# Out projection of a decoder layer: sets of 256 features in two half banks, or sets of 512 with a block of tokens in each bank

## The chip, the cores and the metric

The kernel runs on one core of a Trainium2 chip. The metric is the device time of one execution in microseconds (us). A core has five engines with queues of their own: TensorE (PE, matrix products; PEld is its weight load), VectorE (DVE), ScalarE (ACT), GpSimd (POOL) and SyncE (SP, which here issues nearly all DMAs). Products go to PSUM, which has eight banks of 128 x 512 float32.

## The reference

One decoder layer on 512 tokens of 2048 features, in float32. A mixer (pooling and attention, merged by gates) gives `merged`; the part around the change is

```
x = x + gate_a * (merged @ w_out)                      # w_out: 2048 x 2048
h = rmsnorm(x, norm_moe) * (1 + scale_m) + shift_m
logits = h @ w_router                                  # 16 experts
# top-2 experts of the best group, for each token
x = x + gate_m * sum_of_experts(h)
out = rmsnorm(x, norm_final)
```

The kernel keeps float32 accuracy with three products for each one: an operand is split into a high part (`hi`, rounded to the type fp32r) and a rest (`lo`), and hi x hi, hi x lo and lo x hi are summed.

## The kernel before

All of the program is a list of items (`Item`) that `run_items` walks through. An item has `split` (ScalarE writes the high part of 128x1024 weights, VectorE the rest; `split_tiles`), `mm` (its products) and lists of functions that come `before` the products, `now` (right behind them) or `after` (before the next item's products, behind the next split). With `split_ahead` 1 the order in which instructions are written out is: split of item i+1, `after` of item i-1, products of item i, `now` of item i, split of item i+2, `after` of item i, and so on. Every engine works its own instructions in that order. Two sets of split weights alternate (`parts`), so the split of item i+2 begins when the products of item i are over. Weights come in loads of 1 MB into three buffers in turn (`ring`); a load serves two items.

The out projection (`out_items`, `pair_items` with `token_major`) takes the 2048 output features 256 at a time: eight sets p of four items, 48 products an item. A stationary block is 128 tokens of `hh` or `hl` (the split `merged`); what streams is 256 columns of `w_out`, so a product is 128x256 (lines L645, L647, L648). A set has two banks, each of which holds two blocks of tokens side by side; sets alternate between banks 0, 1 and banks 2, 3 (`next_pair`). The set's `post` comes behind the next set's first splits: for each half, VectorE multiplies the bank by the row of `gate_a` (`ga`, L1049), adds x (`xr`, L1050), multiplies by the norm's row (`am`, L1051), and ScalarE sums the squares into `ssq2` (L1053). Two DMAs of 512 KB store z in `zrows` and the new x in `acc` (L1059). In the next set's items z is transposed (`z_turn`, L1068, copied by ScalarE, L1069), and the router's logits are summed (`logits`, L1077). The last set does this at once, half by half. x's columns are loaded a set ahead (`x_load`, L1037, L1040) by SyncE.

Meanwhile eight of the first expert's weight loads (1 MB each, L1154, L1155) go into tiles `craw`, one at every third item (`prefetch`). After the last logits comes the routing, a chain of small VectorE operations, at whose end GpSimd gathers the first expert's rows from `zrows` (L1213), and then 16 experts with weights streamed from memory (L1132, L1133, L1147).

The two lines that set where a set's evacuation stands and which banks it uses:

```
        items[-1].after.append(lambda: post(cell["ps"]))
        rot.update(ids=[0, 1], i=0)
```

Of the kernel before, what the change touches and what calls it, by code (L numbers as in the profile page):

```python
# [21 lines left out]
NB = T // P  # L22
KD = D // P
H = 8
E = 16
# [113 lines left out]
def trunk_kernel(ctx: ExitStack, tc: tile.TileContext, x, c, w_ada, b_ada, norm_mix, norm_moe, w_in,  # L139
# [32 lines left out]
    ssq2 = glob.tile([P, NB * 8], F32, name="ssq2")  # L172
# [55 lines left out]
    def bank(i):  # L228
        return psB.tile([P, 512], F32, name=f"bank{i}", tag=f"bank{i}")
# [404 lines left out]
                mm3(ps.tiles[j], hi[:, js], lo[:, js], mh[:, k + kk, :], ml[:, k + kk, :], k + kk == 0,  # L634
                    k + kk == nk - 1)

    def token_major(ps, k, hi, lo, ws, mh, ml, nk):

        for b in range(NB):
            o, bs = ps.tiles[b // 2][:, (b % 2) * 256:(b % 2) * 256 + 256], slice(b * P, (b + 1) * P)  # L640
            for kk in range(4):
                js = slice(ws[kk], ws[kk] + 256)
                sh, sl = mh[:, k + kk, bs], ml[:, k + kk, bs]

                pe.matmul(o, lhsT=sh, rhs=hi[:, js], start=k + kk == 0 and b % 2 == 0, stop=False,  # L645
                          skip_group_check=True)
                pe.matmul(o, lhsT=sh, rhs=lo[:, js], start=False, stop=False, skip_group_check=True)  # L647
                pe.matmul(o, lhsT=sl, rhs=hi[:, js], start=False, stop=k + kk == nk - 1, skip_group_check=True)  # L648

    def pair_items(w, col0, mh, ml, post, nk=KD, products=feature_major):  # L650

        items, cell = [], {}
        for q in range(nk // 8):
            def load(r, q=q):
                sp.dma_start(r.rearrange("p (k c) -> p k c", c=256),
                             w[q * 1024:(q + 1) * 1024, col0:col0 + 256].rearrange("(k p) c -> p k c", p=P))
                return r

            raw = Raw(load, 2)
            for hf in range(2):  # L660
                def split(raw=raw, hf=hf, q=q):
                    cell[q, hf] = split_tiles(raw.tile[:, hf * 1024:(hf + 1) * 1024], 1024)

                def mm(hf=hf, q=q):
                    if q == 0 and hf == 0:
                        cell["ps"] = next_pair()
                    hi, lo = cell.pop((q, hf))
                    products(cell["ps"], q * 8 + hf * 4, hi, lo, [0, 256, 512, 768], mh, ml, nk)
# [325 lines left out]
        slot += 1  # L994


    c_stack = ctx.enter_context(ExitStack())
    b3_stack = ctx.enter_context(ExitStack())
    b3, c_ = {}, {}
    lg_pair = {}  # L1000

    def open_b3():
        am_stack.close()
        g_stack.close()
        b3["pool"] = b3_stack.enter_context(tc.tile_pool(name="b3pool", bufs=1, side="left", reuse_waits="tile"))
        rot.update(ids=[0, 1], i=0)
        lg_pair["t"] = pair(3)
        c_["pool"] = c_stack.enter_context(tc.tile_pool(name="cpool", bufs=1, side="right", reuse_waits="tile"))
        c_["sh"] = c_["pool"].tile([P, D], F32, name="shrow")
        c_["gm"] = c_["pool"].tile([P, D], F32, name="gmrow")  # L1010
        for i, n in enumerate(("sh", "gm")):
            m = modd[i:i + 1].rearrange("s k p -> s (k p)")
            sp.dma_start(c_[n], m.to_broadcast([P, D]))

    def shift_logits():

        w3 = b3["pool"].tile([P, KD, E], F32, name="wshift")
# [9 lines left out]
    def b3_tile(name, n=1024):  # L1027
        return b3["pool"].tile([P, n], F32, name=name, tag=name, bufs=1)

    def out_items(p):  # L1030

        cell = {}
        ps_ = slice(p * 256, (p + 1) * 256)

        def x_load():
            cell["xr"] = xr = b3_tile("xr")
            sp.dma_start(xr.rearrange("p (b c) -> p b c", b=NB), x2d[:, ps_].rearrange("(b p) c -> p b c", p=P))  # L1037
            for i, n in ((2, "ga"), (3, "am")):
                cell[n] = b3_tile(n, 256)
                sp.dma_start(cell[n], modd[i:i + 1].rearrange("s k p -> s (k p)")[:, ps_].to_broadcast([P, 256]))  # L1040

        def post(ps):
            x2, z = cell["xr"], b3_tile("z")
            cell["z"] = z
            for hf in range(2):
                xs_ = slice(hf * 512, (hf + 1) * 512)
                v = {n: t[:, xs_].rearrange("p (b c) -> p b c", c=256) for n, t in (("x2", x2), ("z", z))}
                row = {n: cell[n][:, None, :].to_broadcast([P, 2, 256]) for n in ("ga", "am")}
                dve.tensor_tensor(v["z"], ps.tiles[hf].rearrange("p (b c) -> p b c", c=256), row["ga"], ALU.mult)  # L1049
                dve.tensor_add(x2[:, xs_], x2[:, xs_], z[:, xs_])  # L1050
                dve.tensor_tensor(v["z"], v["x2"], row["am"], ALU.mult)  # L1051
                for b in (2 * hf, 2 * hf + 1):
                    act.activation(b3_tile("junk", 256), x2[:, b * 256:(b + 1) * 256], AF.Square,  # L1053
                                   accum_out=ssq2[:, b * 8 + p:b * 8 + p + 1])
                if p == 7:
                    z_turn(hf)
                    logits(hf)
            for t, d in ((z, zrows), (x2, acc)):
                sp.dma_start(d[0:T, ps_].rearrange("(b p) c -> p b c", p=P), t.rearrange("p (b c) -> p b c", b=NB))  # L1059

        def z_turn(hf):

            ps, zT = bank(4 + hf), b3_tile(f"zT{hf}", 512)
            cell["zT", hf] = zT
            for j in range(2):
                for b in range(2):
                    o = (2 * hf + b) * 256 + j * P
                    pe.transpose(ps[:, (2 * j + b) * P:(2 * j + b + 1) * P], cell["z"][:, o:o + P], ident)  # L1068
            act.activation(zT, ps, AF.Copy)  # L1069

        def logits(hf):
            lg = lg_pair["t"][:, 512:512 + NB * E]
            for b in (2 * hf, 2 * hf + 1):
                for j in range(2):
                    k = 2 * p + j
                    o = (2 * j + b % 2) * P
                    pe.matmul(lg[:, b * E:(b + 1) * E], lhsT=cell["zT", hf][:, o:o + P],  # L1077
                              rhs=wr[:, k, :], start=k == 0 and b == 0, stop=k == KD - 1,
                              skip_group_check=True)

        it = pair_items(wout, p * 256, hh, hl, post, products=token_major)
        return it, x_load, z_turn, logits

    outs = [out_items(p) for p in range(8)]
    b3_items = []
    for p in range(8):
        it = outs[p][0]
        if p == 0:
            gates[-1].after += [open_b3, outs[0][1]]
        else:  # L1090
            for hf in range(2):
                it[1].after.append(lambda f=outs[p - 1][2], hf=hf: f(hf))
                it[2].after.append(lambda f=outs[p - 1][3], hf=hf: f(hf))
            it[1].after.append(outs[p][1])
        b3_items += it
    b3_items[0].after.append(shift_logits)
    b3_items[2].after.append(shift_sum)

    NCR, LSC, LEAD = 8, 2, 4
# [4 lines left out]
    def craw_tile(i):  # L1104
        return c_["pool"].tile([P, 2048], F32, name=f"craw{i}")
# [338 lines left out]
    dve.tensor_reduce(s4, ssq2.rearrange("p (b k) -> p b k", k=8), axis=AX.X, op=ALU.add)  # L1444
    newton_rstd(rs2, s4, t4)
    act.activation(sqrt_set, epst, AF.Exp)
    lg = rtile("lg")
# [279 lines left out]
```

## Time and profile before

| | |
|---|---|
| median of 3 runs | 2397.55 us (2397.06 to 2399.11) |
| the profiled execution | 2397.21 us, of it span 2395.5 us |
| TensorE busy | 2325.1 us, 97% of the span |
| VectorE, ScalarE busy | 1748.3 us, 1163.7 us |
| out projection | 1024.7 to 1227.8 us, TensorE busy 203.10 us |
| routing | 1227.8 to 1255.4 us |
| experts | 1255.4 to 2395.5 us |
| mean granted TensorE clock | 0.988 |

Span is from the first to the last instruction of the profiled execution. Busy time is a union over an engine's instructions. [...]

### The profile page before, as it was taken

The page shows a single profiled execution, that of the slowest core. Times are in us where ns is not written, and L with a number is a line of the kernel's source. Part 1 is how long each engine was busy: PE and PEld are TensorE (multiplying, and loading weights), DVE is VectorE, ACT ScalarE, POOL GpSimd, SP SyncE. Part 2 cuts the span into 40 slices and gives each one's busy share as a digit, 9 for nine tenths or more (in the row PEclk, how much of TensorE's full clock was granted, in tenths as well). Part 3 has the DMA queues.
Part 4 walks back from the last instruction along what each step waited for, and adds up shares of the span by engine and source line. Part 5 has one row for each costly group of instructions (what it writes and reads, how often), then busy time and mean ns, then how long its engine had stood idle before and what let it go on. Part 6 is the DMA issues. An engine that isn't in the chain of part 4 may idle for free.

```text
span 2395.5 us, 29296 instructions
## 1 busy us (share of the span) xinstructions
PE 2325.1 (97%) x11478; PEld 1929.4 (81%) x11478; DVE 1748.3 (73%) x1750; ACT 1163.7 (49%) x1070; POOL 127.7 (5%) x73
## 2 busy tenths in 40 slices
PE   7999999999999999999969999999999999999996
PEld 6888777788887888899968888888788888888883
DVE  7987333377665666343349999999999999999995
ACT  4323323322222222233227777777776777777775
POOL 0000100000000000000000111001101100100010
PEclk9999999999999999999979999999999999999998
DMA  9878724266665667366648999999998999999996
GB/s 338 277 245 205 101 71 71 71 234 240 237 233 192 236 233 256 108 201 196 222 152 314 347 372 384 399 384 368 371 381 345 376 411 366 372 378 376 376 359 264
DMA packets 269775, 662.57 MB, mean 277 GB/s; under 512 B 20084, under 2 KB 160620, under 8 KB 249708
## 3 DMA queue, kind: packets, MB, share of 16 engines
q1 hardware_dynamic: 262112, 641.89, 73.6%
q0 software_dynamic: 4752, 17.48, 3.0%
q8 instruction: 91, 1.49, 0.2%
q10 hardware_dynamic: 2768, 1.29, 0.2%
q14 instruction: 52, 0.43, 0.0%
HBM read 648.32 MB, written 29.39 MB: 283 GB/s over the span
## 4 chain that ended last, share of the span: by engine, by line
PE 77%; DMA 11%; DVE 7%; issue 3%; ACT 2%; POOL 0%; SPq 0%; POOLq 0%; DVEq 0%; ACTq 0%
PE bank L1147 27%; PE bank L242 10%; PE bank L244 10%; PE bank L243 10%; DMA G<-zrows,dest 4%; DVE clo L1133 3%; PE bank L645 3%; PE bank L647 3%; PE bank L648 3%; DMA craw<-in_w_exp_gate_dram 2%; DMA craw<-in_w_exp_down_dram 2%; DVE y L1275 1%; PE bank L1238 1%; ACT chi L1132 1%; PE bank L386 1%
## 5 line engine op out<-in xcount | busy, mean ns | idle before, releaser
L1133 DVE TENSOR_TENSOR clo<-craw,chi 128x2048 fp32r<-128x2048 f32 x270 | 615.7, 2289 | 53.4 <-ACT chi L1132 51.1
L1132 ACT ACTIVATE chi<-craw 128x2048 fp32r<-128x2048 f32 x270 | 518.0, 1920 | 218.3 <-PE bank L1147 202.2
L238 DVE TENSOR_TENSOR wlo<-raw,whi 128x1024 fp32r<-128x1024 f32 (+2 forms) x180 | 213.3, 1185 | 421.4 <-ACT whi L237 387.5
L237 ACT ACTIVATE whi<-raw 128x1024 fp32r<-128x1024 f32 (+2 forms) x180 | 184.6, 1027 | 653.6 <-PE bank L243 356.3
L242 PE MATMUL bank<-hh,whi 128*128 128x512 f32 x846 | 335.5, 397 | 1.4 <-ACT hh L406 1.3
L244 PE MATMUL bank<-hh,wlo 128*128 128x512 f32 x846 | 330.8, 391 | 1.6 <-DVE wlo L238 1.6
L243 PE MATMUL bank<-hl,whi 128*128 128x512 f32 x846 | 330.3, 390 | 0.3 <-DVE hl L410 0.3
L1147 PE MATMUL bank<-chi,xh 128*128 128x512 f32 x1020 | 288.4, 397 | 0.0
L1147 PE MATMUL bank<-clo,xh 128*128 128x512 f32 x1020 | 280.9, 389 | 0.1
L1147 PE MATMUL bank<-chi,xl 128*128 128x512 f32 x1020 | 280.7, 389 | 0.0
L1147 PE MATMUL bank<-chi,glp 128*128 128x512 f32 x992 | 255.4, 389 | 0.3 <-DVE glp L1268 0.3
L1147 PEld LDWEIGHTS bank<-clo,xh 128*128 128x128 f32 x1020 | 191.4, 188 | 41.1 <-DVE clo L1133 0.5
L1147 PEld LDWEIGHTS bank<-chi,xl 128*128 128x128 f32 x1020 | 191.5, 188 | 40.3
L1147 PEld LDWEIGHTS bank<-chi,glp 128*128 128x128 f32 x992 | 186.1, 188 | 39.6 <-DVE glp L1268 0.9
L1147 PEld LDWEIGHTS bank<-chi,xh 128*128 128x128 f32 x1020 | 185.7, 188 | 34.4
L244 PEld LDWEIGHTS bank<-hh,wlo 128*128 128x128 f32 x846 | 159.2, 188 | 36.7 <-DVE wlo L238 3.1
L242 PEld LDWEIGHTS bank<-hh,whi 128*128 128x128 f32 x846 | 159.4, 188 | 35.3 <-ACT hh L406 1.5
L243 PEld LDWEIGHTS bank<-hl,whi 128*128 128x128 f32 x846 | 159.4, 188 | 33.4 <-issue 1.0
L906 DVE SCALAR_TENSOR_TENSOR acc<-raw,cact,acc 128x1024 f32<-128x1024 f32 x120 | 154.0, 1283 | 11.1 <-DMA raw<-in_w_ada_dram 8.5
L645 PE MATMUL bank<-whi,hh 128*128 128x256 f32 x512 | 146.0, 285 | 0.0
L647 PE MATMUL bank<-wlo,hh 128*128 128x256 f32 x512 | 144.8, 283 | 0.0
L648 PE MATMUL bank<-whi,hl 128*128 128x256 f32 x512 | 144.8, 283 | 0.0
(393 smaller groups left out, 3218.5 us busy)
## 6 DMA issues: line engine op xcount, KB each, us to landing
craw<-in_w_exp_down_dram SPq DMA_DIRECT2D x114, 1024.0 KB, 13.3
raw<-in_w_ada_dram SPq DMA_DIRECT2D x82, 1024.0 KB, 6.1
craw<-in_w_exp_gate_dram SPq DMA_DIRECT2D x161, 512.0 KB, 9.9
craw<-in_w_exp_up_dram SPq DMA_DIRECT2D x161, 512.0 KB, 10.0
raw<-in_w_gate_dram SPq DMA_DIRECT2D x32, 1024.0 KB, 5.7
raw<-in_w_branch_dram SPq DMA_DIRECT2D x16, 1024.0 KB, 5.0
raw<-in_w_out_dram SPq DMA_DIRECT2D x16, 1024.0 KB, 9.3
raw<-in_w_in_dram SPq DMA_DIRECT2D x14, 1024.0 KB, 10.7
```

What stands on the lines that cost most here:

```text
L237: act.activation(hi[:, :n], raw[:, :n], AF.Copy)
L238: dve.tensor_tensor(lo[:, :n], raw[:, :n], hi[:, :n].bitcast(F32), ALU.subtract)
L242: pe.matmul(o, lhsT=whi, rhs=xhi, start=first, stop=False)
L243: pe.matmul(o, lhsT=whi, rhs=xlo, start=False, stop=False)
L244: pe.matmul(o, lhsT=wlo, rhs=xhi, start=False, stop=last)
L645: pe.matmul(o, lhsT=sh, rhs=hi[:, js], start=k + kk == 0 and b % 2 == 0, stop=False, skip_group_check=True)
L647: pe.matmul(o, lhsT=sh, rhs=lo[:, js], start=False, stop=False, skip_group_check=True)
L648: pe.matmul(o, lhsT=sl, rhs=hi[:, js], start=False, stop=k + kk == nk - 1, skip_group_check=True)
L906: dve.scalar_tensor_tensor(cell["a"], r, s, cell["a"], op0=ALU.mult, op1=ALU.add)
L1132: act.activation(hi, raw, AF.Copy)
L1133: dve.tensor_tensor(lo, raw, hi.bitcast(F32), ALU.subtract)
L1147: pe.matmul(ps.tiles[n], lhsT=rows, rhs=w[:, n * 512:(n + 1) * 512], start=first and i == 0, stop=last and i == 2)
```

## The change

The out projection takes 512 features at a time: four sets of eight items, 24 products of 128x512 an item (`block`). A load of weights has 512 rows of 2 KB instead of 1024 rows of 1 KB and is still 1 MB. Each of the four blocks of tokens has a bank of its own; every set uses banks 0 to 3. The multiplication by `ga`, which empties a bank, is written out in `now` of the set's last item, block by block, ahead of the split of the set's second item to come. The rest (`added`: x added, norm's row, squares, two stores of 256 KB for each block) follows in the next set's first two items, and transposes and logits in its items 1 to 5, a block at a time. In the last set the products of the last two chunks of 256 input features are ordered by block (`last_chunks`), with the evacuation, transposes and logits of earlier blocks between them. x is loaded into a tile of 1 MB, `x2`, which serves as the eighth `craw` afterwards; so the eighth early expert load is issued behind the last item and not at the 25th.

```diff
-    def token_major(ps, k, hi, lo, ws, mh, ml, nk):
...
-        rot.update(ids=[0, 1], i=0)
+        c_["x2"] = craw_tile(NCR - 1)
...
+        ps_ = slice(p * 512, (p + 1) * 512)
         def x_load():
+            sp.dma_start(c_["x2"].rearrange("p (b c) -> p b c", b=NB), x2d[:, ps_].rearrange("(b p) c -> p b c", p=P))
...
+        def gated(b):
+            if b == 0:
+                cell["z"] = b3_tile("z", 2048)
+            dve.tensor_tensor(z_part(b), cell["ps"][b], cell["ga"], ALU.mult)
+
+        def added(b):
+            x2, z = c_["x2"][:, b * 512:(b + 1) * 512], z_part(b)
+            dve.tensor_add(x2, x2, z)
+            dve.tensor_tensor(z, x2, cell["am"], ALU.mult)
+            act.activation(b3_tile("junk", 512, 1, BF16), x2, AF.Square, accum_out=ssq2[:, b * 4 + p:b * 4 + p + 1])
+            for t, d in ((z, zrows), (x2, acc)):
+                sp.dma_start(d[b * P:(b + 1) * P, ps_], t)
+
+        def z_turn(b):
+            ps = bank(4 + b % 2)
+            cell["zT", b] = zT = b3_tile("zT", 512, 2)
+            for j in range(4):
+                pe.transpose(ps[:, j * P:(j + 1) * P], z_part(b)[:, j * P:(j + 1) * P], ident)
+            act.activation(zT, ps, AF.Copy)
...
+        def block(b, chunks):
+            o, bs = cell["ps"][b], slice(b * P, (b + 1) * P)
+            for c in chunks:
+                hi, lo = cell[c]
+                for kk in range(2):
+                    k, js = 2 * c + kk, slice(kk * 512, (kk + 1) * 512)
+                    pe.matmul(o, lhsT=hh[:, k, bs], rhs=hi[:, js], start=k == 0, stop=False)
+                    pe.matmul(o, lhsT=hh[:, k, bs], rhs=lo[:, js], start=False, stop=False)
+                    pe.matmul(o, lhsT=hl[:, k, bs], rhs=hi[:, js], start=False, stop=k == KD - 1)
+
+        def last_chunks():
+            for b in range(NB):
+                block(b, (6, 7))
+                gated(b)
+                added(b)
+                if b > 0:
+                    z_turn(b - 1)
+                if b > 1:
+                    logits(b - 2)
+            z_turn(NB - 1)
+            logits(NB - 2)
+            logits(NB - 1)
...
+                def mm(c=2 * q + hf):
+                    if c == 0:
+                        cell["ps"] = [bank(i) for i in range(NB)]
+                    if p == 3 and c >= 6:
+                        if c == 7:
+                            last_chunks()
+                        return
+                    for b in range(NB):
+                        block(b, (c,))
...
+            b3_items[-1].now += [lambda b=b, f=gated_: f(b) for b in range(NB)]
+            for b in range(NB):
+                it[b // 2].after.append(lambda b=b, f=added_: f(b))
+                it[b + 1].after.append(lambda b=b, f=z_turn_: f(b))
+                it[b + 2].after.append(lambda b=b, f=logits_: f(b))
+            it[2].after.append(outs[p][1])
...
-        craws.append(craw_tile(len(craws)))
+        craws.append(craw_tile(len(craws)) if len(craws) < NCR - 1 else c_["x2"])
...
-        b3_items[3 + 3 * i].after.append(lambda i=i: prefetch(c_items[i]))
+        b3_items[3 + 3 * i if i < NCR - 1 else -1].after.append(lambda i=i: prefetch(c_items[i]))
```

## Rows read from the trace of the kernel before

**Rows 1.** Stretches: length, busy of PE, PEld, DVE, ACT, POOL, PEclk, DMA share, GB/s.
```profile
1024.70:1227.80 203.10, 203.10 (x1708) 203.06 (x1707) 74.87 (x89) 58.91 (x113) 0.00 (x0) 1.00 0.59 187
1227.80:1255.40 27.60, 9.45 (x53) 8.11 (x51) 14.71 (x57) 5.63 (x13) 5.19 (x12) 0.56 0.66 235
1255.40:2395.50 1140.10, 1108.68 (x5028) 900.18 (x5028) 1041.23 (x723) 811.87 (x541) 105.55 (x32) 0.99 0.92 366
```

**Rows 2.** Groups of instructions by line and form, 1024.7 to 1233.6 us.
```profile
L645 PE MATMUL bank<-whi,hh 128*128 128x256 f32 x512 | 146.0, 285 | 0.0
...
L238 DVE TENSOR_TENSOR wlo<-raw,whi 128x1024 fp32r<-128x1024 f32 x31 | 38.0, 1226 | 117.7 <-ACT whi L237 106.9 <-DMA am<-modd 10.8
L237 ACT ACTIVATE whi<-raw 128x1024 fp32r<-128x1024 f32 x31 | 32.7, 1055 | 108.6 <-PE bank L648 106.7 <-PE bank L243 1.8
...
L1049 DVE TENSOR_TENSOR z<-bank,ga 128x512 f32<-128x512 f32 x16 | 11.0, 685 | 9.7 <-PE bank L648 9.7
```

**Rows 3.** TensorE in order of time (start, duration), 13th product after the first.
```profile
1061.23 0.28 PE L645 MATMUL bank<-whi,hh 128*128 128x256 f32 x1
...
1062.67 0.28 PE L645 MATMUL bank<-whi,hh 128*128 128x256 f32 x1
```

**Rows 4.** The same view, 512-wide: branch stage (three products apart), first expert.
```profile
1016.04 0.39 PE L242 MATMUL bank<-bh,whi 128*128 128x512 f32 x1
...
1016.72 0.39 PE L242 MATMUL bank<-bh,whi 128*128 128x512 f32 x1
...
1270.07 1.07 PE L1147 MATMUL bank<-chi,xh 128*128 128x512 f32 x4
...
1272.79 0.61 PE L1147 MATMUL bank<-chi,xh 128*128 128x512 f32 x2
```

**Rows 5.** The same view: transposes and logits between products, one of seven times.
```profile
1110.99 1.03 PE L1068 MATMUL bank<-ident,z 128*128 128x128 f32 x8
1111.78 0.36 PE L645 MATMUL bank<-whi,hh 128*128 128x256 f32 x1
...
1117.62 1.85 PE L1077 MATMUL bank<-wr,zT 128*128 128x16 f32 x16
1119.32 0.36 PE L645 MATMUL bank<-whi,hh 128*128 128x256 f32 x1
```

**Rows 6.** All engines in order of time, end of the last set.
```profile
1225.16 0.69 DVE L1049 TENSOR_TENSOR z<-bank,ga 128x512 f32<-128x512 f32 x1 [8.96 <-PE bank L648]
...
1227.72 0.28 PE L648 MATMUL bank<-whi,hl 128*128 128x256 f32 x1
...
1228.04 0.69 DVE L1049 TENSOR_TENSOR z<-bank,ga 128x512 f32<-128x512 f32 x1 [0.73 <-PE bank L648]
...
1229.12 1.07 PE L1077 MATMUL bank<-wr,zT 128*128 128x16 f32 x8 [0.69 <-ACT zT L1069]
...
1230.33 0.63 PE L1068 MATMUL bank<-ident,z 128*128 128x128 f32 x4
...
1231.64 1.89 PE L1077 MATMUL bank<-wr,zT 128*128 128x16 f32 x8 [0.69 <-ACT zT L1069]
...
1233.57 0.23 DVE L1448 TENSOR_TENSOR lg<-bank,rs 128x64 f32<-128x64 f32 x1 [0.88 <-PE bank L1077]
```

**Rows 7.** VectorE in order of time, end of the last branch set.
```profile
1027.09 1.28 DVE L950 TENSOR_TENSOR gS<-bank,gS 128x512 f32<-128x512 f32 x2
```

**Rows 8.** First of four loads, the gather's issue, a stretch, all gathers' landing (L1213).
```profile
1231.17 1.04 SPq L1154 DMA_DIRECT2D xh<-in_w_exp_gate_dram  x1
...
1244.67 1.27 POOL L1213 DMA_INDIRECT G<-zrows,dest  x1 [7.49 <-DVE place L1510]
...
1246.00:1249.00 3.00, 0.25 (x2) 0.16 (x1) 1.91 (x9) 0.00 (x0) 0.00 (x0) 0.50 0.80 233
...
DMA to landing us min/median/max: 6.6/9.0/12.0
```

**Rows 9.** SyncE's waits (in all, times, longest); landing of weight loads, 1000 to 1060.
```profile
SPq L1037 <- DMA acc<-xr: 13.4, 7, 4.1
...
DMA to landing us min/median/max: 4.9/8.4/12.8
```

More of the change, by code (lines that the diff above doesn't have):

```diff
@@ L171, in trunk_kernel @@
     rstd = glob.tile([P, NB], F32, name="rstd")
-    ssq2 = glob.tile([P, NB * 8], F32, name="ssq2")
+    ssq2 = glob.tile([P, NB * 8], F32, name="ssq2")[:, 0:NB * 4]
     wr = glob.tile([P, KD, E], F32, name="wr")
@@ L635, in feature_major, with pair_items @@
                     k + kk == nk - 1)
-    def token_major(ps, k, hi, lo, ws, mh, ml, nk):
[L639 to L650, printed above, removed]
+    def pair_items(w, col0, mh, ml, post, nk=KD):
         items, cell = [], {}
@@ L667, in mm @@
                     hi, lo = cell.pop((q, hf))
-                    products(cell["ps"], q * 8 + hf * 4, hi, lo, [0, 256, 512, 768], mh, ml, nk)
+                    feature_major(cell["ps"], q * 8 + hf * 4, hi, lo, [0, 256, 512, 768], mh, ml, nk)
                 items.append(Item(raw, split, mm))
@@ L994, in trunk_kernel, with craw_tile @@
         slot += 1
+    NCR, LSC, LEAD = 8, 2, 4
+    def craw_tile(i):
+        return c_["pool"].tile([P, 2048], F32, name=f"craw{i}")
     c_stack = ctx.enter_context(ExitStack())
@@ L1015, in shift_logits @@
     def shift_logits():
-        w3 = b3["pool"].tile([P, KD, E], F32, name="wshift")
+        w3 = b3_tile("z", 2048)[:, 0:KD * E].rearrange("p (k e) -> p k e", e=E)
         dve.tensor_tensor(w3, wr, shiftM[:, :, None].to_broadcast([P, KD, E]), ALU.mult)
@@ L1025, in shift_sum, with b3_tile @@
         dve.tensor_copy(cst, lg_pair["t"][:, 0:E])
-    def b3_tile(name, n=1024):
-        return b3["pool"].tile([P, n], F32, name=name, tag=name, bufs=1)
+    def b3_tile(name, n, bufs=1, dt=F32):
+        return b3["pool"].tile([P, n], dt, name=name, tag=name, bufs=bufs)
     def out_items(p):
-        cell = {}
-        ps_ = slice(p * 256, (p + 1) * 256)
+        cell, items = {}, []
+        ps_ = slice(p * 512, (p + 1) * 512)
         def x_load():
-            cell["xr"] = xr = b3_tile("xr")
-            sp.dma_start(xr.rearrange("p (b c) -> p b c", b=NB), x2d[:, ps_].rearrange("(b p) c -> p b c", p=P))
+            sp.dma_start(c_["x2"].rearrange("p (b c) -> p b c", b=NB), x2d[:, ps_].rearrange("(b p) c -> p b c", p=P))
@@ L1038, in x_load @@
             for i, n in ((2, "ga"), (3, "am")):
[L1039 to L1044, printed above, removed]
-            for hf in range(2):
[L1046 to L1079, printed above, removed]
@@ L1081, in out_items, with z_part @@
-        it = pair_items(wout, p * 256, hh, hl, post, products=token_major)
-        return it, x_load, z_turn, logits
-    outs = [out_items(p) for p in range(8)]
+                cell[n] = b3_tile(n, 512)
+                sp.dma_start(cell[n], modd[i:i + 1].rearrange("s k p -> s (k p)")[:, ps_].to_broadcast([P, 512]))
+        def z_part(b):
+            return cell["z"][:, b * 512:(b + 1) * 512]
+        def gated(b):
+            if b == 0:
+                cell["z"] = b3_tile("z", 2048)
+            dve.tensor_tensor(z_part(b), cell["ps"][b], cell["ga"], ALU.mult)
@@ new lines, in logits @@
+        def logits(b):
+            lg = lg_pair["t"][:, 512:512 + NB * E]
+            for j in range(4):
+                k = 4 * p + j
+                pe.matmul(lg[:, b * E:(b + 1) * E], lhsT=cell["zT", b][:, j * P:(j + 1) * P], rhs=wr[:, k, :],
+                          start=k == 0 and b == 0, stop=k == KD - 1, skip_group_check=True)
+        def block(b, chunks):
[7 more added lines that the diff above has]
+                    pe.matmul(o, lhsT=hl[:, k, bs], rhs=hi[:, js], start=False, stop=k == KD - 1)
@@ new lines, in last_chunks, with load, split @@
+        def last_chunks():
[10 more added lines that the diff above has]
+            logits(NB - 1)
+        for q in range(4):
+            def load(r, q=q):
+                sp.dma_start(r.rearrange("p (k c) -> p k c", c=512),
+                             wout[q * 512:(q + 1) * 512, ps_].rearrange("(k p) c -> p k c", p=P))
+                return r
+            raw = Raw(load, 2)
+            for hf in range(2):
+                def split(c=2 * q + hf, raw=raw, hf=hf):
+                    cell[c] = split_tiles(raw.tile[:, hf * 1024:(hf + 1) * 1024], 1024)
+                def mm(c=2 * q + hf):
[7 more added lines that the diff above has]
+                        block(b, (c,))
+                items.append(Item(raw, split, mm))
@@ L1085, in trunk_kernel @@
+        return items, x_load, gated, added, z_turn, logits
+    outs = [out_items(p) for p in range(4)]
     b3_items = []
-    for p in range(8):
+    for p in range(4):
         it = outs[p][0]
@@ L1090, in trunk_kernel @@
         else:
[L1091 to L1094, printed above, removed]
+            x_load_, gated_, added_, z_turn_, logits_ = outs[p - 1][1:]
+            b3_items[-1].now += [lambda b=b, f=gated_: f(b) for b in range(NB)]
[4 more added lines that the diff above has]
+            it[2].after.append(outs[p][1])
         b3_items += it
@@ L1097, in trunk_kernel @@
     b3_items[2].after.append(shift_sum)
-    NCR, LSC, LEAD = 8, 2, 4
     wg3 = w_exp_gate.rearrange("l e k f -> (l e) k f")
@@ L1102, in trunk_kernel @@
     wd3 = w_exp_down.rearrange("l e f d -> (l e) f d")
-    def craw_tile(i):
-        return c_["pool"].tile([P, 2048], F32, name=f"craw{i}")
     def c_tile(name, shape, dt=F32, bufs=1):
@@ L1443, in trunk_kernel @@
     s4, rs2, t4 = (glob.tile([P, NB], F32, name=n) for n in ("s4", "rs2", "t4"))
-    dve.tensor_reduce(s4, ssq2.rearrange("p (b k) -> p b k", k=8), axis=AX.X, op=ALU.add)
+    dve.tensor_reduce(s4, ssq2.rearrange("p (b k) -> p b k", k=4), axis=AX.X, op=ALU.add)
     newton_rstd(rs2, s4, t4)
```

## The prediction

> **What bounds the kernel now.** I read the stages first, then the groups of the stage that is changed, then its products in order of time. The stages [rows 1]: in the out projection (1024.7 to 1227.8 us) TensorE is busy 203.10 of 203.10 us at full granted clock, VectorE 74.87 and ScalarE 58.91; the DMA share is 0.59. The reader should see that nothing else can end last there: a microsecond less of TensorE's work is a microsecond less of stage. Behind it lie 27.6 us of routing, where TensorE works 9.45 us at clock 0.56, and then the experts, 1140.1 us with TensorE busy 1108.68. Nothing in these two stages is tied to an absolute time: they begin with the last logits and with the gather of the first expert's rows. So a shift of the out projection's end arrives at the kernel's end, unless the change makes the handover itself dearer.
>
> The products: 1536 of 128x256 in three groups of 512, [rows 2] shows one. Their recorded 285 ns is no cost, since records overlap; the cost is the distance of starts. Twelve products from 1061.23 to 1062.67 make 0.120 us each [rows 3], so 1536 make 184.3 us. The rest of the stage is what stands between products, seven times each: 8 transposes (0.79 us) and 16 logit instructions (1.70 us), each followed by a product whose record is 0.08 longer [rows 5]. 7 x 2.65 = 18.6, and 184.3 + 18.6 = 202.9 against 203.1 measured: the stage is explained.
>
> **The change, part by part.**
>
> *Wide products.* 1536 products of 256 columns become 768 of 512. The trace of before has 512-wide ones: three in the gate and branch stage take 0.68 us, 0.2267 each, and 12 in the expert stage, where the weights stream as they will here, take 2.72, again 0.2267 [rows 4]. So 768 x 0.2267 = 174.1 us, **-10.2 us**. Two narrow products take 0.240, one wide one 0.2267: a fixed 13.3 ns per product is paid half as often. [...]
>
> *Transposes and logits between products.* Transposes before the last product stay 56. Of the logits' 112 instructions 8 move behind the last product, -8 x 0.106 = -0.85 (0.106 is 1.70 / 16). Groups become more: five a set for three sets and two in the last, 17 against 14, each with 0.08 for the product after it, +0.24. Together **-0.6**; bounds -0.9 and +0.4, if each returning block of four transposes pays twice that.
>
> *One set of banks instead of two.* Every set now uses banks 0 to 3, so its first products must wait until the gating multiply of the set before has emptied them. Block by block, bank b takes its last product (3 - b) x 6 x 0.2267 = (3 - b) x 1.36 us before the item's end. The multiply is 0.685 us [rows 2] and starts 0.32 us behind the start of the product it waits for (1227.72 and 1228.04 in [rows 6]). Banks 0 to 2 are therefore empty before the next item begins; bank 3 is empty 0.9 us into it and wanted at 4.08. Cost 0. What hides it is that VectorE meets the multiplies ahead of the next split: that split's subtraction is behind them, but waits for ScalarE's 1.06 us first, which starts at the same moment as the fourth multiply, so it isn't late either. Without that order the price is worked out under the rivals. The very first set takes over banks 2 and 3 from the last branch set, whose two reads run from 1027.09 for 1.28 us [rows 7]. The third block wants bank 2 at 1024.88 + 2.72 = 1027.60 and gets it at 1027.73 or a little later: **+0.2**, 0.8 if both reads have to be over.
>
> *VectorE, ScalarE, DMA.* The elementwise work keeps its elements. Per set VectorE has 12 operations of 0.69 and 8 subtractions of 1.23, 18 us of 47: hidden under 8 items of 5.44 us. In the first two items of a set VectorE carries a split (2.3 us with ScalarE's part) and 2.8 us of adds, 5.1 of 5.44, and the transposes that need them come an item later. The weights' loads stay 1 MB each, three in turn: a buffer is free some 24.9 us before its next use (5 items less the 2.3 us of a split); landing takes 12.8 at most [rows 9], so 12 us are spare. SyncE now issues eight stores a set instead of two, and x's load for the next set still waits for a store to land, as it does now (13.4 us in 7 waits, the longest 4.1 [rows 9]); behind it stand weight loads with those 12 us to spare. Cost 0.
>
> *The last set.* Its last two chunks run block after block, so the item before computes nothing and the split of chunk 7 can only begin when chunk 5 is done: 0.2 + 1.06 + 1.23, ready some 2.6 us later. TensorE has the last logits of the set before (0.9), six products (1.36) and one more (0.23): 2.5. **+0.1**, 1.0 if the logits come earlier. After the last product the same three VectorE steps of 512 columns follow, 4 transposes, the copy and 8 logits, as before [rows 6]. Before, the logits' sum is read 5.85 us after the last product's start, 5.73 after its 0.120 slot. After: 0.43 until the multiply (the record is 0.11 longer), 2.29 until the transposes, 1.31 until the last block's logits could start. But block 2's 8 logits now stand ahead of them and take 0.85 to 1.7, and the last 8 take 1.07 at full clock or 1.89 at half, as the two rows show. That is 4.9 to 6.6 us after the 0.227 slot, -0.8 to +0.9. Half clock is what the row at that place has, so I lean there: **+0.4**.
>
> *The eighth early load.* One expert load of 1 MB goes into x's tile, so SyncE waits for the last store to land before it, and four further loads queue behind. They began at 1231.17 [rows 8]; now 2 to 4 us later (a store's landing, as above), and there are five instead of four, but most stores are already done. 5.24 MB are moved from then on, as now with the stores; at the experts' 366 GB/s [rows 1] 14.3 us. The end shifts from about 1245.5 to between 1247.5 and 1249.5, in before's time. The first expert's gather is issued at 1244.67, on the path, and lands after 6.6 us while the loads ebb; the gathers amid loads have a median of 9.0 and a maximum of 12.0 [rows 8]. So 0 to +5.4; it meets the loads for part of its way: half of the way to the median, **+1.2**.
>
> Sum: -10.2 - 0.6 + 0.2 + 0.1 + 0.4 + 1.2 = **-8.9 us**. Against the profiled execution's 2397.21 (span 2395.5 and 1.7 around it) that is 2388.3; the median of the runs, 2397.55, lies 0.3 above that execution, so 2388.6.
>
> **Rivals.**
>
> *The handover is dear.* The sum stands but the gather and the half clock take their upper ends: +5.4 and +0.9 instead of 1.2 and 0.4 make -4.2, 2393.3; at the median of the gathers, 2389.8 to 2390.3. For it: the loads' share is still 0.80 in the slice 1246 to 1249 [rows 8]. Against: they have their peak earlier.
>
> *Wide products gain nothing.* If in the new order (the same stationary block twice running, six products in a row on one bank) a product took 0.240, only the handover's costs would stay: about +1.3, 2398.9, no change. Against: both 512-wide forms have the same 0.2267. [...]
>
> *The four banks change hands as one.* This is the case of the other side. If the first product of a set waits for all four multiplies, and these stand behind the next split's subtraction, then 0.32 + 1.06 + 1.23 + 4 x 0.69 = 5.4 us are lost at each of three changes, 16.1 in all: 2404.7, slower. If they are ahead of the split, 3.1 each, 9.2 in all: 2397.8, no change. It decides the sign above 3.0 us a change. Against it: at 1225.16 the multiply of the first bank began 2.56 us before the last product of the same set [rows 6], so the release goes by bank.
>
> **How the numbers follow.** 0.2% is 4.8 us, about what a measurement of this kernel can tell from no change. My forecast, -7 to -11: 0.65. Dear handover, -4.2 to -7, nearly all of it faster: 0.17. More than -11 (the tail at full clock, nothing lost at the gather): 0.03. No gain of wide products: 0.05. Banks as one: no change 0.05, slower 0.05. So faster 0.85, same 0.10, slower 0.05. Unknowns at their best ends make -10.2 - 0.9 - 0.8 = -11.9, 2385.6; at their worst -10.2 + 0.4 + 0.8 + 1.0 + 0.9 + 5.4 = -1.7, but not all at once. The range is 2385.0 to 2393.5: it takes in the dear gather and leaves out a little over one case in ten.
>
> **What would show it.** Right: 768 wide products 0.2267 apart, no idle TensorE between the first and the last, the out projection 193 to 194 us long, the first multiplies of a set inside its last item. The time from the last product to the logits' sum near 6 us, the gather landing in 6.6 to 9 us, the experts' stage as long as before within 1 us. Wrong: gaps of TensorE at the three changes of set or at the third block of the first item; weight loads landing after they are wanted; a gather of 10 us or more; an expert stage that is longer because its first loads came late.

## The result and the profile after

The changed kernel takes 2381.62 us (median of 4, 2379.16 to 2385.56), the kernel before 2397.31 in the same runs: ratio 0.9936, 95% interval 0.9924 to 0.9948. That is 15.7 us where 8.9 were forecast, outside the range. In a later set of runs of both kernels the ratio was 0.9938 [0.9925, 0.9952]. So the sign is right and the size is not, and the question is where the other 7 us come from.

The stages after (columns as in [rows 1]):

```profile
1021.70:1214.60 192.90, 192.83 (x934) 161.49 (x933) 74.50 (x89) 56.20 (x83) 0.22 (x2) 1.00 0.58 193
1214.60:1242.30 27.70, 10.14 (x60) 9.18 (x58) 14.67 (x57) 5.30 (x11) 4.95 (x12) 0.56 0.71 253
1242.30:2377.40 1135.10, 1107.53 (x5028) 900.24 (x5028) 1040.98 (x723) 811.70 (x541) 107.00 (x32) 0.99 0.93 367
```

The middle row is the routing, as long as before. But the out projection begins 3 us earlier, although nothing ahead of it was edited, and the experts take 5 us less, although nothing there was edited either. (How far these two stages differ between profiles of one and the same kernel follows below.)

Inside the stage, groups by line (answering [rows 2]), then the first products and VectorE's reads of the last branch set in order of time:

```profile
L1071 PE MATMUL bank<-whi,hh 128*128 128x512 f32 x256 | 101.4, 396 | 0.1
...
L1040 DVE TENSOR_TENSOR z<-bank,ga 128x512 f32<-128x512 f32 x16 | 10.8, 688 | 8.8 <-PE bank L1073 8.8
```

```profile
1021.67 0.39 PE L1071 MATMUL bank<-whi,hh 128*128 128x512 f32 x1
1021.90 0.39 PE L1072 MATMUL bank<-wlo,hh 128*128 128x512 f32 x1
...
1024.17 0.39 PE L1073 MATMUL bank<-whi,hl 128*128 128x512 f32 x1
1024.62 0.50 PE L1071 MATMUL bank<-whi,hh 128*128 128x512 f32 x1
```

```profile
1023.88 1.28 DVE L937 TENSOR_TENSOR gS<-bank,gS 128x512 f32<-128x512 f32 x2
```

Twelve products from 1021.67 reach 1024.17 for the last: 2.50 / 11 = 0.227 each. The product at 1024.62 is the third block's first; it comes 0.45 behind its neighbour, 0.22 late, where the prediction put +0.2 for the bank of the last branch set. The first of VectorE's two reads is over halfway, at about 1024.52, just ahead of it, the second only at 1025.16: the wait is for the one bank. All idle time in front of 256 products is 0.1 us: no wait at the three changes of set.

The end of the last set (answering [rows 6]; TensorE and VectorE in order of time):

```profile
1204.56 0.69 DVE L1040 TENSOR_TENSOR z<-bank,ga 128x512 f32<-128x512 f32 x1 [1.52 <-PE bank L1073]
...
1214.58 0.69 DVE L1040 TENSOR_TENSOR z<-bank,ga 128x512 f32<-128x512 f32 x1 [1.93 <-PE bank L1073]
```

```profile
1214.15 0.39 PE L1073 MATMUL bank<-whi,hl 128*128 128x512 f32 x1
1214.38 0.60 PE L1055 MATMUL bank<-ident,z 128*128 128x128 f32 x4
1214.81 0.96 PE L1062 MATMUL bank<-wr,zT 128*128 128x16 f32 x8
1216.86 0.63 PE L1055 MATMUL bank<-ident,z 128*128 128x128 f32 x4 [1.09 <-DVE z L1045]
1217.35 3.19 PE L1062 MATMUL bank<-wr,zT 128*128 128x16 f32 x16
```

The logits' sum is read at 1220.57, 6.42 us behind the last product (5.85 before). The last 16 logits take 3.19 us, 0.2 each, at a mean granted clock of 0.57: most of it is the half clock to which the prediction leaned.

I cut each profile at five events and compared two pairs: the two kernels as first profiled, and both profiled once more on one chip (times in us, after less before):

| stretch | first pair | second pair |
|---|---|---|
| start to first out-projection product | -3.21 | -2.71 |
| first product to the logits' sum | 208.69 to 198.90: **-9.79** | 208.65 to 198.84: **-9.81** |
| logits' sum to first expert product | -0.18 | 0.00 |
| to the last scatter into `acc` | -1.45 | +1.90 |
| from there to the end | -3.47 | -3.78 |
| span | -18.1 | -14.4 |

The second row agrees to 0.02 and the fourth changes its sign, so that one is scatter. The first and the last are gained twice, in code that is the same in both kernels. The experts as a whole scatter by more than the change: the kernel before took 1140.1 us in its first profile and 1134.0 in its second, the kernel after 1135.2 and 1132.2. So the 5 us of the stage table don't tell what the change does there; the last row of this table, gained twice, does.

### The profile page after: what moved, and what is told of

Read it like the earlier page. It is cut to its first block, busy times and chain, and to the rows that moved or that the text cites. A ratio compares the mean times of both kernels' runs of the same rounds, so it can differ in the third digit from the quotient of the medians.

```text
span 2377.4 us, 27745 instructions
## 1 busy us (share of the span) xinstructions
PE 2313.7 (97%) x10710; PEld 1889.2 (79%) x10710; DVE 1747.5 (74%) x1750; ACT 1160.9 (49%) x1038; POOL 136.0 (6%) x73
## 3 DMA queue, kind: packets, MB, share of 16 engines
q8 instruction: 85, 1.39, 0.2%
## 4 chain that ended last, share of the span: by engine, by line
PE 81%; DMA 8%; DVE 6%; issue 2%; ACT 2%; POOL 0%; POOLq 0%; ACTq 0%; DVEq 0%; SPq 0%
PE bank L1175 32%; PE bank L242 10%; PE bank L244 10%; PE bank L243 10%; DMA G<-zrows,dest 4%; PE bank L1071 2%; PE bank L1072 2%; PE bank L1073 2%; DVE clo L1161 2%; DMA craw<-in_w_exp_down_dram 2%; DVE y L1303 1%; PE bank L1266 1%; DMA raw<-in_w_ada_dram 1%; ACT chi L1160 1%; PE bank L732 1%
## 5 line engine op out<-in xcount | busy, mean ns | idle before, releaser
L1175 PE MATMUL bank<-clo,glp 128*128 128x512 f32 x496 | 140.0, 389 | 0.4 <-DVE clo L1161 0.4
L1308 POOL DMA_INDIRECT acc<-y,dest x15 | 74.9, 4993 | 927.2 <-DVE y L1303 927.2
L1175 PEld LDWEIGHTS bank<-clo,glp 128*128 128x128 f32 x496 | 93.0, 188 | 20.1 <-DVE clo L1161 0.9
```

What stands on the lines that cost most here:

```text
L1175: pe.matmul(ps.tiles[n], lhsT=rows, rhs=w[:, n * 512:(n + 1) * 512], start=first and i == 0, stop=last and i == 2)
L1308: gp.indirect_dma_start(out=acc[:], out_offset=bass.IndirectOffsetOnAxis(ap=r_["dest"][:, e:e + 1], axis=0), in_=weigh(e), in_offset=None, ...
```

## The experiments

**Both kernels once more**, five rounds.

> The kernel before, unchanged. The out projection and its tail gave the 10 us that were worked out (first product to the logits' sum 208.7 before, 198.9 after), but the profiled executions also differ by 3.2 us ahead of the out projection, where the two programs are the same, and by 4.9 us in the experts' stage. Theory 1 (these 8 us are scatter from execution to execution, and the kernel after was caught on a good side): this profile starts the out projection anywhere from 1021 to 1026 and has an experts' stage anywhere from 1135 to 1141 us. Theory 2 (they belong to the changed program): start at 1024.9 and experts' stage at 1140, each within 0.7, and times within 2396 to 2400.

> The kernel after, unchanged. Theory 1: with more runs its median rises towards 2387 (the 10.0 us of the out projection alone), and this profile's start of the out projection and experts' stage differ from the first one's by several us. Theory 2: the median stays at 2381.6 within 1.5, the out projection starts at 1021.7 and the experts' stage takes 1135.2, each within 0.7.

Measured: before 2390.18 us (2387.44 to 2391.89), ratio to itself 0.9997 [0.9988, 1.0006]; after 2376.17 (2374.06 to 2377.67), 0.9938 [0.9925, 0.9952], 14 us apart. Theory 1 (scatter of all 8 us) falls: an extra gain repeats, at the same two places (the table's right column). But of Theory 2's numbers only the starts hold (1024.57 and 1021.86); the experts' stages miss theirs by 6 and 3 us, and both medians are lower. It gives the places and no cause.

**Narrow products in the new order.**

```diff
-                    pe.matmul(o, lhsT=hh[:, k, bs], rhs=hi[:, js], start=k == 0, stop=False)
+                    for h2 in range(2):
+                        oo = o[:, h2 * 256:(h2 + 1) * 256]
+                        js = slice(kk * 512 + h2 * 256, kk * 512 + (h2 + 1) * 256)
+                        pe.matmul(oo, lhsT=hh[:, k, bs], rhs=hi[:, js], start=k == 0 and h2 == 0, stop=False,
...
```

> The kernel after with each 128x512 product cut into two of 128x256 on the two halves of the bank, all else kept. If the gain of the out projection is the fixed 13.3 ns of 768 products, the stage gets 10.2 us longer (first product to the logits' sum 209.1 instead of 198.9) and the kernel is 10 us slower than the kernel after. If the gain comes from the order of the evacuation or of the last set, it is slower by less than 3 us.

Measured: 2387.06 us (2384.07 to 2390.16), 0.9986 [0.9977, 0.9995]. From the first to the last product it takes 201.95 us, the kernel after 192.48: the width is worth 9.5 us of stage (to the logits' sum 207.84, where 209.1 was expected). The 10.9 us of median are not the width alone, since this kernel's list of products is as long as before's (see the products that never run). The rows of before, which gave 10.2 us for the width, fit to 0.7 us.

**Evacuation behind the split.**

```diff
-            b3_items[-1].now += [lambda b=b, f=gated_: f(b) for b in range(NB)]
+            b3_items[-1].after += [lambda b=b, f=gated_: f(b) for b in range(NB)]
```

> The kernel after with the multiplies that empty the banks written out behind the next split, where the kernel before had its evacuation. If the place ahead of the split is what makes one set of banks free of cost, TensorE waits some 3 us at each of three changes of set: the out projection 9 us longer (about 208), most of the gain gone. If release by bank hides it anyway, less than 1 us.

Measured: 2386.38 us (2384.25 to 2389.66), 0.9985 [0.9975, 0.9994], 10.2 above the kernel after. Its longest waits in the stage (in all, times, longest):

```profile
PE bank L1071 <- DVE z L1040: 9.3, 3, 3.1
```

TensorE waits 3.1 us at each of the three changes, and from the first to the last product it takes 204.14 us, 11.7 more. So the new single set of banks is free only because the multiplies stand ahead of the split: the cover that the prediction named is the one.

**The last set in the plain order.** Products chunk by chunk, then all four blocks' work behind the last one.

```diff
-                block(b, (6, 7))
...
-                    if p == 3 and c >= 6:
-                        if c == 7:
-                            last_chunks()
-                        return
...
+            items[-1].now.append(last_chunks)
```

> The kernel after with the last set in the order of the others: all its products chunk by chunk, and then, behind the last one, the four blocks' multiplies, additions, transposes and logits. Theory A (the order by blocks hides three blocks' work of VectorE behind the products): the time from the last product to the logits' sum is 5.5 to 6.5 us longer than 6.4, that is 12 to 13 us, and the kernel 5 to 6 us slower than the kernel after. Theory B (the chain of a single block, transposes and logits at half clock, sets the tail either way): 7 to 8 us, and no measurable change.

Measured: 2379.09 us (2377.82 to 2382.72), 0.9943 [0.9927, 0.9960]; from the first product to the logits' sum 199.31 us against 198.84 and 198.90. My 5.5 to 6.5 us was wrong, and Theory B's 7 to 8 us from the last product to the sum too (8.91):

```profile
1210.31 0.69 DVE L1040 TENSOR_TENSOR z<-bank,ga 128x512 f32<-128x512 f32 x1 [5.38 <-PE bank L1073]
...
1217.92 0.69 DVE L1045 TENSOR_TENSOR z<-craw,am 128x512 f32<-128x512 f32 x1
```

The last chunk already goes block by block, so the first bank is full 4 us ahead of the last product (1213.96), and VectorE's twelve steps end 4.7 us behind it. The products meanwhile end 2 us earlier, since no transposes stand between them. The special order of the last set is worth 0.4 to 0.8 us of the stage (198.50 to 198.90 in the six profiles that have it), too little for the medians to tell.

**The eighth early load alone**, in the kernel before.

```diff
-        b3_items[3 + 3 * i].after.append(lambda i=i: prefetch(c_items[i]))
+        b3_items[3 + 3 * i if i < NCR - 1 else -1].after.append(lambda i=i: prefetch(c_items[i]))
```

> The kernel before with only the eighth early load of the experts' weights moved from the 24th item to behind the last one. By the prediction's term: the first gather lands later, the routing and the first products of the experts 1.2 us later (23.1 us from the logits' sum to the first expert product in place of 21.6 to 21.9). By what the profile after shows: nothing, 21.6 to 21.9 us, ratio to the kernel before 1.000.

Measured: 2388.87 us (2383.71 to 2391.81), 0.9988 [0.9978, 0.9997]. The first gather lands after 7.7 us instead of 6.6, and the first expert product comes 22.06 us behind the logits' sum: +0.2 to +0.5, not +1.2. In the kernel after it lands after 6.8. (In the variants of the kernel after, which load it as late, the stretch takes 21.72 to 22.84 us and the gather 6.6 to 8.4, so now and then about 1 us is lost there.) This run also had a last scatter 0.84 us behind VectorE, not 3.3, though nothing of the end was touched; the next experiments tell why.

**One instruction of GpSimd.** In the kernel before, the last scatter (POOL) starts 3.29 us after VectorE finished its rows, in the kernel after 0.84. In that wait no engine works, and one packet of 8 KB arrives (10 GB/s x 0.8 us). It is on the queue q14, which the page calls instruction (52 packets, 0.43 MB); TensorE's instructions have another, q8: it has 91 packets in the kernel before and the narrow one, and 85 in the kernel after, which executes 768 products fewer. Kernel before, VectorE and GpSimd in order of time, three stretches, and the only queue with traffic in the wait:

```profile
2384.20 1.28 DVE L1333 SCALAR_TENSOR_TENSOR xh<-xh,er,nf 128x1024 f32<-128x1024 f32 x1
2388.77 1.02 POOL L1334 DMA_INDIRECT out_dram<-xh,dest  x1 [53.00 <-issue]
```

```profile
2385.50:2386.50 1.00, 0.00 (x0) 0.00 (x0) 0.00 (x0) 0.00 (x0) 0.00 (x0) 0.50 0.00 0
2386.50:2387.30 0.80, 0.00 (x0) 0.00 (x0) 0.00 (x0) 0.00 (x0) 0.00 (x0) 0.50 0.04 10
2387.30:2388.70 1.40, 0.00 (x0) 0.00 (x0) 0.00 (x0) 0.00 (x0) 0.00 (x0) 0.50 0.00 0
```

```profile
q14 instruction: 1, 0.01, 1.1%
```

Kernel after, the same two instructions:

```profile
2368.55 1.29 DVE L1361 SCALAR_TENSOR_TENSOR xh<-xh,er,nf 128x1024 f32<-128x1024 f32 x1
2370.68 1.02 POOL L1362 DMA_INDIRECT out_dram<-xh,dest  x1 [49.56 <-DVE xh L1361]
```

The built programs differ by one: 207 instructions of GpSimd before, 208 after (one more semaphore wait at the start of the routing; the traces hold the executed ones, 184 and 185). So I added one to the kernel before and took one from the kernel after.

```diff
# before_pool1, in the kernel before
     gp.memset(striu, 1.0)
+    gp.memset(striu, 1.0)
# after_pool0, in the kernel after
-    gp.memset(striu, 1.0)
+    dve.memset(striu, 1.0)
```

> The kernel before with one instruction more on GpSimd, a memset at the start that is written twice. Theory A (the last scatter waits for GpSimd's next block of 128 instructions, whose first instruction it happens to be; the kernel after has one instruction more ahead of it): the last scatter starts 0.8 to 1.0 us behind the end of VectorE's last write of xh in place of 3.3, the stretch from the last scatter into acc to the end of the span is 74.4 to 74.8 us in place of 77.0 to 77.2, ratio to the kernel before 0.999. Theory B (something else of the changed kernel ends earlier, the store queue or the clock at the end): 3.3 and 77 stay.

> The kernel after with one instruction fewer on GpSimd (that memset at the start is VectorE's). Theory A: the last scatter starts 3.3 us behind VectorE's last write of xh, where it was 0.84, and the stretch from the last scatter into acc to the end is 75.6 to 76.2 us in place of 73.2 to 73.7; some 2.4 us slower than the kernel after. Theory B: 0.84 and 73.2 to 73.7 stay.

Measured: 2389.17 us (2384.43 to 2391.87), 0.9995 [0.9985, 1.0004], and 2380.60 (2376.12 to 2384.73), 0.9952 [0.9934, 0.9970]. The intervals are too wide for 2.4 us; the traces are not. Kernel before with one more:

```profile
2373.86 1.28 DVE L1334 SCALAR_TENSOR_TENSOR xh<-xh,er,nf 128x1024 f32<-128x1024 f32 x1
2375.99 1.01 POOL L1335 DMA_INDIRECT out_dram<-xh,dest  x1 [49.01 <-DVE xh L1334]
```

Kernel after with one fewer:

```profile
2368.19 1.28 DVE L1361 SCALAR_TENSOR_TENSOR xh<-xh,er,nf 128x1024 f32<-128x1024 f32 x1
2372.61 1.02 POOL L1362 DMA_INDIRECT out_dram<-xh,dest  x1 [49.52 <-issue]
```

One memset at the start of the program moves the last scatter from 3.29 to 0.85 us behind VectorE, and back from 0.84 to 3.14. Every run has or lacks the wait as Theory A says: with 207 instructions it is 3.05 to 3.29 (four profiles), with 208 it is 0.84 or 0.85 (nine). In the four a packet of q14 arrives 1.1 to 1.2 us behind VectorE's end; in the nine the last one is there 4 us and more ahead of it. The run of the eighth load has 208 as well; its extra instruction stands in a loop that is never entered (184 executed, as in the kernel before). That the scatter is the first instruction of a block of 128, as the theory has it, no run shows by itself. The 128 is my estimate: 8 KB hold 128 instructions if these are as long as TensorE's, which come 256 to a packet of 16 KB (1536 instructions and 6 packets fewer on q8 in the kernel after). So it is also my reading that the scatter waits for this packet; the packet's time and the switch by one instruction are what was measured. The whole stretch from the last scatter into `acc` fits less well: 73.21 where 74.4 to 74.8, and 79.13 where 75.6 to 76.2 were expected; other parts of it scatter (the program's last products among them, see what stays open).

**Products that never run.** What moves the start of the out projection? The largest single step between the two kernels stands at 229 us, in the mixer. ScalarE, kernel before, then after:

```profile
228.81 1.16 ACT L237 ACTIVATE whi<-bh 128x520 fp32r<-128x520 f32 x2 [5.00 <-DMA bh<-in_w_in_dram]
```

```profile
227.51 0.64 ACT L237 ACTIVATE whi<-bh 128x520 fp32r<-128x520 f32 x1 [3.25 <-DVE bl L535]
```

Before, a weight load lands late, and TensorE idles 1.0 us behind it; after, it doesn't. TensorE in the kernel before:

```profile
229.50 0.39 PE L701 MATMUL bank<-whi,hh 128*128 128x260 f32 x1 [0.66 <-ACT whi L237]
230.24 0.39 PE L702 MATMUL bank<-wlo,hh 128*128 128x260 f32 x1 [0.35 <-DVE wlo L238]
```

The narrow kernel, with TensorE's old number of products, has the late load too (waits of 0.57 and 0.35). So I lengthened the list of the kernel after without executing more:

```diff
# in the loop over further blocks of an expert's tokens, which these data never enter
+                for _ in range(193):
-                pe.matmul(ps[:, 0:4], lhsT=oh[:, b * P:(b + 1) * P], rhs=val4[:, b, :], start=b == 0,
-                          stop=b == NB - 1)
+                    pe.matmul(ps[:, 0:4], lhsT=oh[:, b * P:(b + 1) * P], rhs=val4[:, b, :], start=b == 0,
+                              stop=b == NB - 1, skip_group_check=True)
# pad_half: range(97)
```

> The kernel after with 768 products more in the loop over further blocks of an expert's tokens, which these data never enter: TensorE's list of instructions is as long as in the kernel before, none more is executed. Theory A (part of the time saved ahead of the out projection comes from where things lie when the list is shorter): the wait of ScalarE for a weight load at 229 us comes back and the first product of the out projection is 1.6 us later than in the kernel after, 1023.3 to 1023.5 (its start apart, which scatters by 2 us). Theory B (scatter, or something that runs): no such wait, 1021.7 to 1021.9 and the time of the kernel after.

> As the padded kernel, with 384 products that never run in place of 768. Theory A (any other length of the list gives other landing times of the same loads): the waits ahead of the out projection differ from those at 0 and at 768, between none and 2.7 us at 225 to 231 us. Theory B (the length matters by how much is added): half of the 1.6 us that 768 cost, some 0.8 us.

Measured: 2378.04 us (2376.63 to 2386.30), 0.9947 [0.9932, 0.9962], and 2381.83 (2380.27 to 2384.17), 0.9956 [0.9938, 0.9973]. Both intervals hold the kernel after's 0.9938, so the medians don't tell; the traces do. With 768 more, ScalarE and TensorE:

```profile
228.78 1.17 ACT L237 ACTIVATE whi<-bh 128x520 fp32r<-128x520 f32 x2 [6.81 <-DMA bh<-in_w_in_dram]
```

```profile
225.92 0.39 PE L689 MATMUL bank<-wlo,hh 128*128 128x260 f32 x1 [1.66 <-DVE wlo L238]
229.47 0.39 PE L688 MATMUL bank<-whi,hh 128*128 128x260 f32 x1 [0.54 <-ACT whi L237]
230.21 0.39 PE L689 MATMUL bank<-wlo,hh 128*128 128x260 f32 x1 [0.35 <-DVE wlo L238]
```

The late load is back. It is the load of `bh` issued at 218 to 220 us; from issue to landing, kernel after, then with 768 more:

```profile
DMA to landing us min/median/max: 7.8/7.8/7.8
```

```profile
DMA to landing us min/median/max: 10.3/10.3/10.3
```

With the short list it takes 7.4 to 8.5 us (five profiles of four kernels), with a longer one 9.3 to 10.9 (six). For the kernel before itself the landing isn't recorded, but ScalarE waits for it until 9.5 and 9.4 us after the issue. TensorE's waits from 225 to 235 us are none in the kernel after, 0.66 + 0.35 = 1.01 us in the kernel before, 2.54 with 768 more, 0.50 + 0.35 = 0.85 with 384 more. Of the 2.54 us, 1.66 are due to the load of `bh` before this one, for which VectorE waits too. So 384 more cost about what the kernel before loses with its full list, and no half of what 768 more cost: Theory B of that run hit its 0.8 us by chance, and the loss does not grow with the length alone.

The late load is not all. One product of the mixer (the 1027th; at 221.90 us in the kernel before, 222.35 after) starts between 220.0 and 223.4 us in the thirteen profiles, by scatter of the first 60 us (the 0.45 us between these two kernels is there at the 201st product already, 58.06 against 58.56). From it to the first product of the out projection, 3667 products further on and the same ones in every kernel, the time depends on TensorE's list. The two products in the kernel before, then in the kernel after, whose second one is shown above at 1021.67:

```profile
221.90 0.28 PE L701 MATMUL bank<-whi,hh 128*128 128x260 f32 x1
...
1024.88 0.28 PE L645 MATMUL bank<-whi,hh 128*128 128x256 f32 x1
```

```profile
222.35 0.28 PE L688 MATMUL bank<-whi,hh 128*128 128x260 f32 x1
```

| TensorE's list | profiles | from the 1027th product to the out projection |
|---|---|---|
| short (the kernel after and three of its variants) | 5 | 799.2 to 800.2 us |
| as before (the kernel before, two variants, narrow) | 5 | 802.5 to 803.0 |
| short, and 384 or 768 products that never run | 3 | 803.4 to 803.9 |

The groups don't overlap, and each chip of the record (8, 0 and 15) has profiles in two or three of them. So instructions that are never executed changed when this load landed (7.8 us after its issue without them, 9.3 with 384 and 10.3 with 768), and in the kernel after 384 or 768 of them cost 3.2 to 4.7 us ahead of the out projection; by what rule, these runs don't settle.

**Both taken back**: the kernel after with 768 products that never run and one GpSimd instruction fewer (both diffs above).

> The kernel after with both accidents of its instruction lists taken back: one instruction fewer on GpSimd, and 768 products that never run in TensorE's list. Theory A (the out projection is worth 9.8 us, the rest of the gain is where instructions lie): the wait for a weight load at 229 us and the 3.1 us ahead of the last scatter are both back, the stage of the out projection stays 198.5 to 198.9 us, and the gain on the kernel before shrinks from 14 to 8.5 to 10.5 us, ratio 0.9956 to 0.9964. Theory B (the gain beyond the out projection has other causes): 14 us, 0.994.

Measured: 2385.45 us (2379.37 to 2390.78), 0.9966 [0.9955, 0.9976]. The gain shrinks to 7.2 us by the medians, 5.7 to 10.8 by the interval, while the stage of the out projection stays 198.50. The waits are back (2.33, 0.57 and 0.35 us from 229 to 233 us, 2.2 us more than before's) and the last scatter is 3.05 us behind VectorE. Theory B's 14 us is excluded; the 8.5 to 10.5 of Theory A lie within the interval, above the median.

## Why the prediction was wrong, and where it was right

**The step that failed** is in its first part: "Nothing in these two stages is tied to an absolute time ... So a shift of the out projection's end arrives at the kernel's end", with its test that the experts' stage be as long as before within 1 us, and, unsaid, that the code ahead of the change keeps its time. Apart from the eighth load, the program outside the stage was put at nothing, and for the code ahead of it no reason was given. What the edit changed there is not the work but the instruction lists. TensorE's is 768 products shorter, and the out projection begins 3.66 and 2.93 us sooner behind the 1027th product in the two pairs, 1.4 to 1.6 of it at the late load. GpSimd's is one longer, and 2.2 to 2.4 us go at the last scatter. The two parts make 5 to 6 of the 6.5 to 6.7 us that the first and last row of the table gain; each came back when only its list was changed. The test itself could not have been met: the experts' stage of the kernel before alone differs by 6 us between two profiles.

**The sum inside the stage was right, in part by luck.** The terms down to the logits' sum made -10.1; measured -9.79 and -9.81. *Wide products*, transposes, bank and split: -10.5 forecast from the first to the last product, -10.36 measured (202.84 to 192.48). But the narrow kernel divides this differently from the prediction: the width gives -9.5 (192.48 against 201.95) where -10.2 was put, and the new order at the old width gives -0.9 (201.95 against 202.84) where the other terms made -0.3. The two misses cancel. *Tail*: +0.4 forecast, +0.57 measured (6.02 to 6.15 us instead of 6.42 in the four later profiles with this end, so +0.2 to +0.6). *First bank*: +0.2 and 0.22.

**The eighth early load was mis-sized.** +1.2 forecast; in the two kernels -0.18 and 0.00 from the logits' sum to the first expert product, alone +0.2 to +0.5, and up to about +1 in the variants. The loads do start later: xh's at 1221.98, 7.8 us behind the last product, before 3.45 [rows 6, 8]. But the gather lands after 6.8 us, not near the 9.0 of gathers amid loads. Without this term the forecast would have been -10.1, still short of the 14 to 15.7 us measured.

**The rivals.** The dear handover did not come, nor did equal wide and narrow products. Banks as one did not come either: the kernel after has no wait at the changes of set. Even with the evacuation behind the split the wait is 3.1 us, near the 0.32 + 1.06 + 1.23 + 0.69 = 3.3 of the first bank alone and not the 5.4 of all four; so there too the release goes by bank.

**Open.** How landing times follow the length of a list. Behind the late load the short list gains another 1.8 to 2.2 us up to the out projection, in steps of 0.2 to 1.4 us at 510, 620 and 890 us, where other weights' splits come less late; 384 products that never run take back all of this, 768 only 0.2 to 1.2 us. The last 26 products of the last expert: 13.6 to 13.8 us in five profiles (mean granted clock 0.84 in the kernel before) and 12.3 to 12.6 in eight (0.91 in the kernel after). No edit explains which, and it is 1 us of the difference at the end.

## What to carry to other kernels

Cost a stage by the distance of starts of the same form in the trace, and find the work that hides a moved step by name: that gave this stage to 0.3 us, with two terms off by 0.6 to 0.7 that cancelled. Then, for a gain of a few microseconds, allow several more (here 5 to 6) in either direction for what the edit does to instruction lists elsewhere, and compare stage by stage before crediting the edit. Look at the last wait of the program: here it ended in "issue", with a packet of the queue instruction in it, and one instruction more ahead of it shortened it from 3.29 us to 0.85.

## What the runs showed of the hardware

- The last scatter started 3.05 to 3.29 us behind VectorE with 207 instructions of GpSimd (four profiles), with a packet of 8 KB on a queue called instruction in that wait, and 0.84 or 0.85 us with 208 (nine). A single instruction 2.3 ms earlier switched it, or (the eighth load alone) one that is never executed.
- The queue q8, called instruction too, moved 91 packets, 1.49 MB, in the kernel before and 85, 1.39 MB, in the kernel after, 16 KB each: 6 packets fewer for 768 products and as many weight loads fewer, so 256 instructions each.
- 384 and 768 products that never run moved one load's landing from 7.8 us after its issue to 9.3 and 10.3, and TensorE's waits there from none to 0.85 and 2.54 us. Over the 800 us up to the out projection they cost 3.2 to 4.7 us.
